# Projections beside the samples' cache pages: small factors, page weights and half of each page sum move from SBUF to PSUM, and the samples' softmax is reordered

## The chip, the cores and the metric

One core of a Trainium2 chip runs the whole program in one launch. The metric is device microseconds of that core, the median of several runs. Engines are called as in the profile: PE (TensorE), DVE (VectorE), ACT (ScalarE), POOL (GpSimd) and SP (SyncE, which issues most DMAs). Each engine takes its own instructions in the order written; engines wait for one another through semaphores.

## What is computed

The program is one step of a two-layer decoder for a prompt of 1024 tokens and for 8 samples of one token each. The change lies in the part between the two layers, where queries, keys, values and a gate are projected and where the samples attend to their cached pages. Cut to that part, the reference is:

```python
def shared_kv(x, kv_norm, kv_w, kv_fb, k_norm):
    u = rmsnorm(x, kv_norm) @ kv_w
    k = rmsnorm(u[..., :ATTN_DIM].reshape(b, t, N_HEADS, HEAD_DIM), k_norm)
    v = u[..., ATTN_DIM:2 * ATTN_DIM].reshape(b, t, N_HEADS, HEAD_DIM)
    logf = jax.nn.log_sigmoid((u[..., 2 * ATTN_DIM:] + kv_fb).astype(jnp.float32))
...
past_k = cache_k[page_table].reshape(bs, -1, N_HEADS, HEAD_DIM)   # 8 samples x 8 pages x 128 rows
past_v = cache_v[page_table].reshape(bs, -1, N_HEADS, HEAD_DIM)
...
def fox_mixer(x, k, v, cq, ck, q_pos, k_pos, norm_g, w_in, q_g, w_out):
    u = rmsnorm(x, norm_g) @ w_in
    q = rmsnorm(u[..., :ATTN_DIM].reshape(b, t, N_HEADS, HEAD_DIM), q_g)
    z = u[..., ATTN_DIM:]
    o = fox_attend(q, k, v, cq, ck, q_pos, k_pos).reshape(b, t, ATTN_DIM)   # softmax(q k / sqrt(d) + C[t] - C[s]) v
    return x + (o * jax.nn.silu(z)) @ w_out
```

There are 16 heads of 64 columns; a page holds 128 rows of 1024 columns of float32.

## The kernel before

The program has four stretches: the convolution layer (to about 467 us), the projections (467 to 973 us), the prompt's attention, and the output projection. The change touches the second.

**Eight steps of the projections.** `KINDS` names them: queries, keys, values and gate, each in two halves of 512 columns. Call them steps 0 to 7. Steps 0 to 5 run over eight tiles of 128 tokens; a tile is 24 matmuls of 512 columns into one PSUM bank (`pq`, L1105 to L1107). Its eight weight pieces (`wp`) are split into a high and a low part by ACT (L807) and DVE (L808) one step ahead, and the samples' own rows (`sample`, L883 and L884, 16 matmuls) come first in each step. Steps 6 and 7 (`gate`, L1053 to L1055) make the gate, four column blocks each.

**A tile's tail.** For queries and keys ACT copies the bank to `qn`, `head_rstd` makes eight factors per token (squares on ACT, L826; four small operations on DVE, L827, L830 to L832, with Ln and Exp on ACT between them), DVE multiplies the tile by them (L858), and three tiles later PE transposes the result (`ptq`, L872). For values ACT copies the bank to `vo`, and ACT (L848) and DVE (L849) split it into `vx`, which has two buffers and goes out by DMA.

**The samples' pages** run beside this. `keys` loads a page half (`kh`), multiplies it by the sample's query (L906; every fourth on DVE, the rest on POOL) and reduces it on DVE to logits in `lg` (L907). `softmax` turns the logits of four samples into weights, with small matmuls on PE between DVE's operations (`pm`, L984, L988, L998; `pd`, L1013). `values` loads both halves of a page (`vt`), multiplies them by the page's weights on DVE (L683) and adds them to `av` (L685; three quarters on POOL, a quarter on DVE); when a sample's eight pages are in, `fold` sums the rows by eight matmuls on PE (`pv`, L668). Samples 0 to 5 do this here, 6 and 7 in the output projection.

**The order.** `later_work` is a list of generators of which `pump2` takes APUMP[step] pieces (a page each) after each tile and ZPUMP after each block of the gate; `side` holds generators that advance by one piece at each `tick`. A scheduler then orders each engine's instructions by its own estimate of times. All eight PSUM banks of the stretch belong to one pool of eight (`psB1`).

Of the kernel before, what the change touches and what calls it, by code (L numbers as in the profile page):

```python
# [66 lines left out]
AP2 = 4  # L67
AP3 = 3
AP4 = 3
# [4 lines left out]
TLAG = 3  # L74
KHB = 6
# [24 lines left out]
ST = 2  # L100
# [34 lines left out]
def tile_step(ctx, tc, xt, st, stT, vecs, cwT, win, wout, wqkv, wf, wbo, hvec, qgf, ck, cv, cf, pt,  # L135
# [525 lines left out]
    def values(a, b, pool, kb, ab, bank):  # L661
        def fold(s_, av):
            while not bank:
                yield
            yield from [None] * FT
            pv = bank[0]("pv")
            for k in range(KT):
                PE.matmul(pv[:, k:k + 1], av[:, k * P:(k + 1) * P], ones[:, 0:1], start=True, stop=True)  # L668
            V.tensor_tensor(out=oT[:, :, s_], in0=pv[:, 0:KT], in1=oT[:, :, s_], op=ALU.add)
            folded.append(s_)  # L670

        for s_ in range(a, b):
            while s_ // 4 not in done or s_ - ab >= a and s_ - ab not in folded:
                yield
            av = pool.tile([P, D], F32, tag="av", name="av", bufs=ab)
            for g in range(NPG):
                i = s_ * NPG + g
                vt = [pool.tile([P, 512], F32, tag="kh", name="vt", bufs=kb) for _ in range(2)]
                fetch(i, *[(vt[x], cv, slice(x * 512, x * 512 + 512)) for x in range(2)])
                for x in range(2):  # L680
                    ax = av[:, x * 512:x * 512 + 512]
                    p0 = i * NH + x * 8
# [22 lines left out]
    with ExitStack() as pb:  # L705
# [6 lines left out]
        psB = pb.enter_context(tc.tile_pool(name="psB1", bufs=8, space=PSUM, reuse_waits="tile"))  # L712
# [21 lines left out]
        def gates():  # L734
            lfx = big("lfx")
            yield
            for o, n in CH:
# [7 lines left out]
                yield  # L745
            pl = bank("pl")
# [72 lines left out]
        def head_rstd(src, pn, nh, out):  # L819
            n = nh * HD  # L820
            sq = pX.tile([P, 512], F32, tag="hsq", name="hsq", bufs=2)
            v = sm.tile([P, 8], F32, tag="hv", name="hvv")
            y = sm.tile([P, 8], F32, tag="hv", name="hvy")
            a = sm.tile([P, 8], F32, tag="hv", name="hva")
            for h in range(nh):
                S.activation(out=sq[:pn, 0:HD], in_=src[:, h * HD:(h + 1) * HD], func=AF.Square, accum_out=v[:pn, h:h + 1])  # L826
            V.tensor_scalar(out=v[:pn, :nh], in0=v[:pn, :nh], scalar1=1.0 / HD, scalar2=EPS, op0=ALU.mult, op1=ALU.add)  # L827
            S.activation(out=y[:pn, :nh], in_=v[:pn, :nh], func=AF.Ln)
            S.activation(out=y[:pn, :nh], in_=y[:pn, :nh], func=AF.Exp, scale=-0.5)
            V.scalar_tensor_tensor(out=a[:pn, :nh], in0=y[:pn, :nh], scalar=-0.5, in1=y[:pn, :nh], op0=ALU.mult, op1=ALU.mult)  # L830
            V.tensor_tensor(out=a[:pn, :nh], in0=a[:pn, :nh], in1=v[:pn, :nh], op=ALU.mult)
            return V.scalar_tensor_tensor(out=out, in0=a[:pn, :nh], scalar=1.5, in1=y[:pn, :nh], op0=ALU.add, op1=ALU.mult)  # L832
# [3 lines left out]
        def token_tile(kind, half, t, ps):  # L836
            cs = slice(half * 512, (half + 1) * 512)
            if kind == 2:
                vo = wk.tile([P, 512], F32, tag="qn", name="vo", bufs=QNB)
                S.copy(out=vo, in_=ps)  # L840
                for x in range(2):

                    vx = pY.tile([P, 512], F32R, tag="tn", name="vx", bufs=TNB).rearrange("p (h a d) -> p h a d", h=4, a=2)
                    vi = heads(vo[:, x * 256:x * 256 + 256])
# [11 lines left out]
            r = sm.tile([P, 8], F32, tag="hr", name="hr")  # L856
# [22 lines left out]
        def sample(kind, half, ws):  # L879
# [9 lines left out]
            if kind < 2:  # L889
                r = sm.tile([P, 8], F32, tag="hr", name="hrs")  # L890
# [6 lines left out]
        def keys(half, a=0, b=NS):  # L897
            cs = slice(half * 512, (half + 1) * 512)
            for s_ in range(a, b):
                qb = pY.tile([P, 512], F32, tag="qb", name="qb", bufs=3)  # L900
                SY.dma_start(out=qb, in_=qs_scr[s_:s_ + 1, cs].broadcast_to([P, 512]))
                for g in range(NPG):
# [3 lines left out]
                    (V if g % 4 == 3 else G).tensor_tensor(out=kt, in0=kt, in1=qb, op=ALU.mult)  # L906
# [65 lines left out]

        def softmax(hf):
# [7 lines left out]
            yield from [None] * ST  # L981
# [4 lines left out]
            yield from [None] * ST  # L986
# [9 lines left out]
            yield from [None] * ST  # L996
# [14 lines left out]
            yield from [None] * ST  # L1011
# [22 lines left out]
        def new_row():  # L1034
            while not lns:
                yield
            ln = lns[0]
            nv = sample_rows(2)
            V.tensor_tensor(out=heads(nv), in0=heads(nv), in1=over_d(ln, NS, NH), op=ALU.mult)
            yield from [None] * NRT  # L1040
            pot = bank("pot")
            for k in range(KT):
                PE.transpose(pot[:, k * NS:(k + 1) * NS], nv[:, k * P:(k + 1) * P], ident[:NS, :NS])
# [25 lines left out]

        def started(hf):  # L1070

            while len(pieces_) < 4:
                yield
            side.append(softmax(hf))
# [5 lines left out]
        for n_, (kind, half) in enumerate(order):  # L1080
# [4 lines left out]
            if kind == 3:  # L1085
                if half:
                    pR.close()
                    load0()
                gate(half, ws)
                continue  # L1090
            sample(kind, half, ws)
            pieces_.append(n_)
            if n_ == 0:
                gate_work = gates()
                later_work.extend([page_gates(), keys(0)])
            if n_ == 1:
                later_work.extend([keys(1, 0, 4), started(0), keys(1, 4, NS), started(1), values(0, VB, pW, KHB, AVB, [bank])])
            if n_ == 2:
                side.append(page_bias())
            if n_ == 5:  # L1100
                side.append(new_row())
            for t in range(8):
                ps = bank("pq")
# [314 lines left out]
```

## Time and profile before

| | us |
|---|---|
| median of 3 runs | 1462.08 |
| runs | 1460.68, 1462.08, 1472.82 |
| the profiled execution | 1459.9 |
| its span, first to last instruction | 1458.2 |
| PE busy in it | 1292.8 (89%) |
| DVE, ACT, POOL busy | 1132.5 (78%), 734.1 (50%), 803.9 (55%) |

The span is what the trace shows; the execution's time is 1.7 us more, and the median of the runs is 2.2 us above this execution. Busy shares are means over stretches with different limits. PE's busy time includes time at a lowered clock, which the profile gives as a granted share of full speed.

### The profile page before, as it was taken

How to read it: one execution, taken by the hardware profiler on the slowest of the kernel's cores; microseconds unless marked ns; L12 is line 12 of the kernel's file. 1: busy time of each engine (PE TensorE's matmuls, PEld its weight loads, DVE VectorE, ACT ScalarE, POOL GpSimd, SP SyncE). 2: the span in 40 equal slices, each digit the busy share in tenths (PEclk: the TensorE clock that was granted, in tenths of full speed). 3: DMA queues.
4: the chain of work that ended last, by engine and by line, in shares of the span. 5: the costliest groups of instructions: out<-in, count | busy, mean ns of one | idle time of the engine just before them, and what ended most of it. 6: DMA issues, size and time to landing. Idle time of an engine off the chain costs nothing.

```text
span 1458.2 us, 21461 instructions
## 1 busy us (share of the span) xinstructions
PE 1292.8 (89%) x6543; PEld 1077.8 (74%) x6543; DVE 1132.5 (78%) x1844; ACT 734.1 (50%) x1922; POOL 803.9 (55%) x603
## 2 busy tenths in 40 slices
PE   5999999789999999998898899897988888887978
PEld 5999999777777777666776778786766666665766
DVE  6999999998735699989898999854656575667841
ACT  7676537646645666655642232135656565662100
POOL 4699987862210253456565565724545455567930
PEclk9999999999999999999998989997868798888979
DMA  5111001121334576878778888693444456423841
GB/s 206 56 59 59 30 29 34 30 75 41 130 125 145 158 225 203 229 250 272 231 251 273 277 272 268 211 241 91 111 96 101 92 133 133 101 48 118 286 139 37
DMA packets 155530, 213.95 MB, mean 147 GB/s; under 512 B 14057, under 2 KB 82281, under 8 KB 155399
## 3 DMA queue, kind: packets, MB, share of 16 engines
q1 hardware_dynamic: 137879, 202.09, 47.4%
q10 hardware_dynamic: 16896, 8.39, 2.0%
q0 software_dynamic: 640, 2.10, 0.5%
q8 instruction: 52, 0.85, 0.3%
q14 instruction: 63, 0.52, 0.1%
HBM read 165.22 MB, written 48.13 MB: 146 GB/s over the span
## 4 chain that ended last, share of the span: by engine, by line
PE 18%; DMA 10%; DVE 10%; issue 5%; SPq 4%; ACT 2%; POOL 1%; DVEq 0%; ACTq 0%; POOLq 0%
DMA k<-c_scr 4%; DVE vt L683 4%; DMA vt<-in_cv 3%; SPq L639 2%; PE st L1228 2%; PE st L1229 2%; PE ss L1166 2%; PE ss L1165 2%; DMA k<-kt_scr 2%; PE po L1208 1%; PE po L1209 1%; PE py L1312 1%; PE py L1314 1%; PE py L1313 1%; PE pz L1055 1%
## 5 line engine op out<-in xcount | busy, mean ns | idle before, releaser
L347 POOL TENSOR_TENSOR cvt<-cvt 128x512 f32<-128x512 f32 (+4 forms) x179 | 243.7, 1394 | 38.4 <-ACT cvt L343 35.5
L906 POOL TENSOR_TENSOR kh<-kh,qb 128x512 f32<-128x512 f32 x96 | 139.8, 1472 | 135.6 <-DMA kh<-in_ck 85.4
L352 DVE SCALAR_TENSOR_TENSOR acc<-u,cw,acc 128x512 f32<-128x512 f32 (+4 forms) x285 | 196.0, 742 | 0.1
L198 POOL TENSOR_SCALAR ph<-pt 128x896 fp32r<-128x896 f32 (+1 forms) x96 | 87.6, 921 | 175.9 <-ACT pt L1238 172.3
L1169 DVE TENSOR_REDUCE nm<-ss 128x1 f32<-128x768 f32 (+7 forms) x128 | 93.6, 751 | 110.4 <-PE ss L1168 97.5
L685 POOL TENSOR_TENSOR av<-av,vt 128x512 f32<-128x512 f32 x80 | 134.2, 1698 | 69.8 <-DVE vt L683 53.0
L1105 PE MATMUL pq<-wp,acth 128*128 128x512 f32 x384 | 160.1, 417 | 0.0
L1107 PE MATMUL pq<-wp,actl 128*128 128x512 f32 x384 | 156.4, 407 | 0.0
L1106 PE MATMUL pq<-wp,acth 128*128 128x512 f32 x384 | 156.2, 407 | 0.0
L683 DVE TENSOR_TENSOR vt<-vt,lg 128x512 f32<-128x512 f32 x112 | 133.8, 1228 | 7.8 <-DMA vt<-in_cv 7.6
L343 ACT ACTIVATE cvt<-u,cw 128x512 f32<-128x512 f32 (+4 forms) x195 | 126.1, 719 | 17.9 <-POOL cvt L347 9.4
L1171 ACT ACTIVATE ss<-ss,nm 128x768 f32<-128x768 f32 (+7 forms) x128 | 91.2, 713 | 44.5 <-DVE nm L1169 43.4
L1238 ACT ACTIVATE pt<-st 128x896 f32<-128x896 f32 (+1 forms) x96 | 75.4, 809 | 71.7 <-PE st L1229 46.6
L1242 POOL TENSOR_TENSOR pl<-pt,ph 128x384 fp32r<-128x384 f32 (+2 forms) x56 | 105.7, 1894 | 2.7
L1165 PE MATMUL ss<-k,q 128*128 128x512 f32 (+2 forms) x192 | 80.2, 425 | 23.7 <-DMA k<-kt_scr 14.6
L1166 PE MATMUL ss<-k,q 68*128 68x512 f32 (+2 forms) x192 | 74.3, 400 | 20.4 <-DMA k<-c_scr 17.7
L1107 PEld LDWEIGHTS pq<-wp,actl 128*128 128x128 f32 x384 | 75.2, 196 | 19.2 <-issue 0.8
L1105 PEld LDWEIGHTS pq<-wp,acth 128*128 128x128 f32 x384 | 75.8, 197 | 18.0 <-ACT hsq L826 0.8
L1106 PEld LDWEIGHTS pq<-wp,acth 128*128 128x128 f32 x384 | 75.7, 197 | 16.9 <-issue 0.2
L907 DVE TENSOR_REDUCE lg<-kh 128x8 f32<-128x512 f32 x128 | 82.7, 673 | 5.0 <-POOL kh L906 5.0
L1208 PE MATMUL po<-ph,vh 128*128 128x512 f32 x192 | 78.3, 411 | 5.8 <-DVE og L1213 4.0
L1228 PE MATMUL st<-q,k 128*128 128x512 f32 (+1 forms) x192 | 79.5, 422 | 3.0 <-ACT ss L1171 2.9
(337 smaller groups left out, 3788.7 us busy)
## 6 DMA issues: line engine op xcount, KB each, us to landing
kh<-in_ck SPq DMA_DIRECT2D x128, 256.0 KB
vt<-in_cv SPq DMA_DIRECT2D x128, 256.0 KB
wraw<-in_wqkv SPq DMA_DIRECT2D x56, 256.0 KB
wr<-in_win SPq DMA_DIRECT2D x24, 512.0 KB
q<-qt_scr SPq DMA_DIRECT2D x48, 256.0 KB
k<-kt_scr SPq DMA_DIRECT2D x48, 256.0 KB
vt_scr<-vx SPq DMA_DIRECT2D x32, 256.0 KB
vh<-vt_scr SPq DMA_DIRECT2D x16, 512.0 KB
```

Source lines behind the costliest of these rows:

```text
L343: S.activation(out=t[:, :m], in_=u[:, lo + j:hi + j], func=AF.Copy, scale=cw[:, c, j:j + 1])
L347: G.tensor_tensor(out=pacc[:, :m], in0=pacc[:, :m], in1=t[:, :m], op=ALU.add)
L352: V.scalar_tensor_tensor(out=acc, in0=u[:, lo + jd:hi + jd], scalar=cw[:, c, jd:jd + 1], in1=acc, op0=ALU.mult, op1=ALU.add)
L683: V.tensor_tensor(out=heads(vt[x] if g else ax), in0=heads(vt[x]), in1=over_d(lg[:, p0:p0 + 8], P, 8), op=ALU.mult)
L685: (V if g % VDVE == 3 else G).tensor_tensor(out=ax, in0=ax, in1=vt[x], op=ALU.add)
L906: (V if g % 4 == 3 else G).tensor_tensor(out=kt, in0=kt, in1=qb, op=ALU.mult)
L1105: PE.matmul(ps, na.hi(k, t * P, P), ws[k][:, 0:512], start=(k == 0), stop=False)
L1106: PE.matmul(ps, na.hi(k, t * P, P), ws[k][:, 512:1024], start=False, stop=False)
L1107: PE.matmul(ps, na.lo(k, t * P, P), ws[k][:, 0:512], start=False, stop=(k == KT - 1))
L1165: PE.matmul(ss[:, b0:b0 + w], q1[:, qsl], k1[:, b0:b0 + w], start=True, stop=False)
L1228: PE.matmul(st[:, o:o + w], k1[:, js], q1[:, qs], start=(o % 512 == 0), stop=False)
L1242: (G if plo else V).tensor_tensor(out=pl[:, :off], in0=pt_[:, :off], in1=f32(ph[:, :off]), op=ALU.subtract)
```

## The change

It does the following. One PSUM bank (`smb`) takes the small tiles of `head_rstd` and a copy of a sample's page weights; another (`a2`) takes the second half of a sample's page sum, whose additions all go to DVE, those of the first half all to POOL, and ACT copies `a2` back to `av` at the end. The pool for projection banks shrinks from eight to six. In `head_rstd` one of DVE's four small operations becomes a Square on ACT, and what remains reads at most one SBUF tile. The value tile's split reads the projection's bank instead of `vo`. For keys DVE multiplies every eighth page instead of every fourth. The samples' own rows of steps 1 to 5 come after the second tile instead of ahead of the first. The logits of samples 0 to 3 are finished in both halves first, the softmax of them starts when they are in, its pieces stand three ticks apart instead of two (fewer in the gate), and the page counts per tile are 3, 3, 3, 4, 4, 3 instead of 3, 3, 4, 3, 3, 3. The samples' new value row is loaded in two halves of another pool.

```diff
-AP2 = 4
-AP3 = 3
-AP4 = 3
+AP2 = 3
+AP3 = 4
+AP4 = 4
...
+SPOS = 2
...
-ST = 2
+ST = 3
...
-    def values(a, b, pool, kb, ab, bank):
+    def values(a, b, pool, kb, ab, bank, small=None, psA=None):
...
+            wt, w0 = lg, s_ * NPG * NH
+            if small is not None:
+                wt, w0 = small(NPG * NH), 0
+                V.tensor_copy(out=wt, in_=lg[:, s_ * NPG * NH:(s_ + 1) * NPG * NH])
+            a2 = av[:, 512:1024] if psA is None else psA.tile([P, 512], F32, tag="a2", name="a2")
...
-                    V.tensor_tensor(out=heads(vt[x] if g else ax), in0=heads(vt[x]), in1=over_d(lg[:, p0:p0 + 8], P, 8), op=ALU.mult)
+                    ax = a2 if x else av[:, 0:512]
+                    p0 = w0 + g * NH + x * 8
+                    V.tensor_tensor(out=heads(vt[x] if g else ax), in0=heads(vt[x]), in1=over_d(wt[:, p0:p0 + 8], P, 8), op=ALU.mult)
                     if g:
-                        (V if g % VDVE == 3 else G).tensor_tensor(out=ax, in0=ax, in1=vt[x], op=ALU.add)
+                        (V if (g % VDVE == 3 if psA is None else x) else G).tensor_tensor(out=ax, in0=ax, in1=vt[x], op=ALU.add)
                 yield
+            if psA is not None:
+                S.copy(out=av[:, 512:1024], in_=a2)
...
-        psB = pb.enter_context(tc.tile_pool(name="psB1", bufs=8, space=PSUM, reuse_waits="tile"))
+        psB = pb.enter_context(tc.tile_pool(name="psB1", bufs=6, space=PSUM, reuse_waits="tile"))
+
+        psm = pb.enter_context(tc.tile_pool(name="psM", bufs=1, space=PSUM, reuse_waits="tile"))
+        smb = psm.tile([P, 512], F32, name="smb")
...
+            yield
             pl = bank("pl")
...
-            v = sm.tile([P, 8], F32, tag="hv", name="hvv")
-            y = sm.tile([P, 8], F32, tag="hv", name="hvy")
-            a = sm.tile([P, 8], F32, tag="hv", name="hva")
+            v, y2, a = [small(8)[:pn, :nh] for c in "vya"]
+            w, y = [sm.tile([P, 8], F32, tag="hw", name="hw" + c)[:pn, :nh] for c in "vy"]
...
+            V.tensor_scalar(out=w, in0=v, scalar1=1.0 / HD, scalar2=EPS, op0=ALU.mult, op1=ALU.add)
+            S.activation(out=y, in_=w, func=AF.Ln)
+            S.activation(out=y, in_=y, func=AF.Exp, scale=-0.5)
+            S.activation(out=y2, in_=y, func=AF.Square)
+            V.scalar_tensor_tensor(out=a, in0=y2, scalar=-0.5, in1=w, op0=ALU.mult, op1=ALU.mult)
+            return V.scalar_tensor_tensor(out=out, in0=a, scalar=1.5, in1=y, op0=ALU.add, op1=ALU.mult)
...
-                    vi = heads(vo[:, x * 256:x * 256 + 256])
+                    vi = heads(ps[:, x * 256:x * 256 + 256])
...
-            r = sm.tile([P, 8], F32, tag="hr", name="hr")
+            r = small(8)
...
-                    (V if g % 4 == 3 else G).tensor_tensor(out=kt, in0=kt, in1=qb, op=ALU.mult)
+                    (V if g % NPG == 7 else G).tensor_tensor(out=kt, in0=kt, in1=qb, op=ALU.mult)
...
+        def hop(n):
+
+            while n > 0:
+                yield
+                n -= 1 + gating[0]
...
-            yield from [None] * ST
+            yield from hop(ST)
...
-            while len(pieces_) < 4:
+            while len(pieces_) < 4 or hf not in counts or hf and 0 not in done:
                 yield
-            side.append(softmax(hf))
+            yield from softmax(hf)
...
-            if n_ == 1:
-                later_work.extend([keys(1, 0, 4), started(0), keys(1, 4, NS), started(1), values(0, VB, pW, KHB, AVB, [bank])])
...
             for t in range(8):
+                if t == SPOS and n_:
+                    sample(kind, half, ws)
+                    pieces_.append(n_)
+                if t == SPOS and n_ == 1:
+                    later_work.extend([keys(1, 0, 4), counted(0), keys(0, 4, NS), keys(1, 4, NS), counted(1), values(0, VB, pW, KHB, AVB, [bank], small, psA)])
```

Three places show what this does to the engines' order. On DVE, in the tail of a key tile (`hvv`, `hvy`, `hva`, `hr` are the small factors, `smb` the new bank, `hwv` and `hwy` two that stay in SBUF), before:

```order
L827 TENSOR_SCALAR hvv<-hvv 128x8
L830 SCALAR_TENSOR_TENSOR hva<-hvy 128x8
L831 TENSOR_TENSOR hva<-hva,hvv 128x8
L832 SCALAR_TENSOR_TENSOR hr<-hva,hvy 128x8
L858 TENSOR_TENSOR qn<-qn,hr 128x512
L907 TENSOR_REDUCE lg<-kh 128x8 x3
```

and now:

```order
L848 TENSOR_SCALAR hwv<-smb 128x8
L852 SCALAR_TENSOR_TENSOR smb<-smb,hwv 128x8
L853 SCALAR_TENSOR_TENSOR smb<-smb,hwy 128x8
L879 TENSOR_TENSOR qn<-qn,smb 128x512
L928 TENSOR_REDUCE lg<-kh 128x8 x3
```

The row with two SBUF factors into a third (L831) is gone, and each of the others reads one operand from PSUM. On DVE, among the page weights' products of step 5, before:

```order
L849 TENSOR_TENSOR vx<-vo,vx 128x4x64
L683 TENSOR_TENSOR vt<-vt,lg 128x512 x5
L685 TENSOR_TENSOR av<-av,vt 128x512
L849 TENSOR_TENSOR vx<-vo,vx 128x4x64
L683 TENSOR_TENSOR vt<-vt,lg 128x512
L985 TENSOR_REDUCE m_5007<-pm 128x4
```

and now, where a new sample begins:

```order
L691 TENSOR_TENSOR a_9477<-a_9477,vt 128x512
L680 COPY smb<-lg 128x128
L689 TENSOR_TENSOR av<-vt,smb 128x512
L689 TENSOR_TENSOR a_9727<-vt,smb 128x512
L689 TENSOR_TENSOR vt<-vt,smb 128x512
L870 TENSOR_TENSOR vx<-pq,vx 128x4x64
L689 TENSOR_TENSOR vt<-vt,smb 128x512
L691 TENSOR_TENSOR a_9727<-a_9727,vt 128x512
```

The products read the weights from the bank, the sum of the second half (`a_9477`, `a_9727`) stands in PSUM, and one of DVE's additions comes with each page. On PE, at the seam from step 5 to the gate, before:

```order
L1107 MATMUL pq<-wp,actl 128x512
L998 MATMUL pm_10270<-dmm,ones 128x64
L668 MATMUL pv<-ones,av 128x1 x8
L1053 MATMUL pz<-acth,wp 128x512
L1054 MATMUL pz<-actl,wp 128x512
```

and now:

```order
L1148 MATMUL pq<-wp,actl 128x512
L1027 MATMUL pm_10344<-dmm,ones 128x64
L669 MATMUL pv<-ones,av 128x1 x4
L1084 MATMUL pz<-acth,wp 128x512
L1085 MATMUL pz<-actl,wp 128x512
```

The page sum at this seam was the second sample's, and it is the third's now (in two groups of four matmuls, of which the first stands here); the first sample's has moved from after the fifth tile of step 5 to after the third.

## Rows read from the trace of the kernel before

**Rows 1.** Windows: steps 0 to 2, steps 3 to 5, gate. Width, busy us by engine, PEclk, DMA share, GB/s.

```profile
467.00:670.00 203.00, 188.71 (x882) 142.10 (x880) 173.87 (x327) 129.54 (x552) 92.80 (x68) 0.96 0.73 216
670.00:857.00 187.00, 163.45 (x691) 129.02 (x691) 169.55 (x255) 76.65 (x282) 107.86 (x71) 0.91 0.85 265
857.00:973.00 116.00, 107.28 (x679) 96.60 (x680) 95.59 (x110) 23.55 (x54) 64.61 (x39) 0.93 0.82 243
```

**Rows 2.** What PE waited for, 467 to 973 us: total us, times, longest.

```profile
PE pm L998 <- ACT le L994: 7.4, 1, 7.4
PE pz L1055 <- DVE wp L808: 6.9, 1, 6.9
PE ptq L872 <- DVE qn L858: 6.4, 5, 2.9
PE pss L884 <- DVE wp L808: 6.4, 2, 4.0
PE pm L988 <- DVE m L985: 5.8, 2, 4.4
...
PE pl L749 <- DVE lfx L744: 3.5, 1, 3.5
```

**Rows 3.** Groups of instructions, 467 to 973 us: busy us, mean ns, idle before.

```profile
L906 POOL TENSOR_TENSOR kh<-kh,qb 128x512 f32<-128x512 f32 x96 | 139.8, 1472 | 135.6 <-DMA kh<-in_ck 85.4 <-DMA qb<-qs_scr 23.4 <-DVE lgw L765 8.1
L685 POOL TENSOR_TENSOR av<-av,vt 128x512 f32<-128x512 f32 x60 | 101.0, 1704 | 66.7 <-DVE vt L683 49.9 <-PE pz L1055 10.0 <-DVE av L685 2.5
L683 DVE TENSOR_TENSOR vt<-vt,lg 128x512 f32<-128x512 f32 x84 | 93.2, 1135 | 7.1 <-DMA vt<-in_cv 6.8
...
L858 DVE TENSOR_TENSOR qn<-qn,hr 128x512 f32<-128x512 f32 x32 | 28.4, 888 | 0.7
L906 DVE TENSOR_TENSOR kh<-kh,qb 128x512 f32<-128x512 f32 x32 | 28.3, 885 | 1.6 <-DMA qb<-qs_scr 1.6
...
L849 DVE TENSOR_TENSOR vx<-vo,vx 128x256 fp32r<-128x256 f32 x32 | 22.0, 693 | 1.8 <-ACT vx L848 1.8
...
L685 DVE TENSOR_TENSOR av<-av,vt 128x512 f32<-128x512 f32 x24 | 20.0, 844 | 1.4 <-POOL av L685 1.2
...
L827 DVE TENSOR_SCALAR hvv<-hvv 128x8 f32<-128x8 f32 x32 | 14.9, 466 | 1.9 <-ACT hsq L826 1.7
...
L831 DVE TENSOR_TENSOR hva<-hva,hvv 128x8 f32<-128x8 f32 x32 | 13.1, 411 | 0.7
...
L830 DVE SCALAR_TENSOR_TENSOR hva<-hvy 128x8 f32<-128x8 f32 x32 | 11.3, 353 | 7.0 <-ACT hvy L829 7.0
L832 DVE SCALAR_TENSOR_TENSOR hr<-hva,hvy 128x8 f32<-128x8 f32 x32 | 10.1, 314 | 0.8
...
L828 ACT ACTIVATE hvy<-hvv 128x8 f32<-128x8 f32 x32 | 6.7, 208 | 62.0 <-DVE hvv L827 58.5 <-DVE hva L831 3.5
```

**Rows 4.** DVE in order of time, 843 to 846 us: start, us.

```profile
843.27 1.78 DVE L683 TENSOR_TENSOR vt<-vt,lg 128x512 f32<-128x512 f32 x1
...
845.05 0.68 DVE L683 TENSOR_TENSOR vt<-vt,lg 128x512 f32<-128x512 f32 x1
```

**Rows 5.** DVE by tile and line: ns min/median/max, first and last start.

```profile
L888 DVE TENSOR_TENSOR sr<-pss,st x6: 671/672/679, 486.2 to 822.5; 8x512 f32<-8x512 f32 x6
...
L669 DVE TENSOR_TENSOR oT<-pv,oT x6: 157/160/173, 845.0 to 962.2; 128x8 f32<-128x8 f32 x6
...
L875 DVE SCALAR_TENSOR_TENSOR tnl<-ptq,qg,tnh x32: 729/739/752, 513.2 to 919.6; 128x512 fp32r<-128x512 f32 x32
...
L849 DVE TENSOR_TENSOR vx<-vo,vx x32: 401/414/1516, 753.8 to 894.7; 128x256 fp32r<-128x256 f32 x32
```

**Rows 6.** Three windows of 15 us, columns as in rows 1.

```profile
485.00:500.00 15.00, 15.00 (x99) 12.66 (x100) 7.81 (x18) 13.81 (x56) 0.00 (x0) 1.00 0.43 128
800.00:815.00 15.00, 15.00 (x67) 12.16 (x66) 15.00 (x19) 5.50 (x9) 8.12 (x5) 1.00 0.96 304
920.00:935.00 15.00, 8.09 (x51) 7.56 (x50) 12.24 (x16) 0.98 (x2) 11.43 (x6) 0.77 0.60 175
```

More of the change, by code (lines that the diff above doesn't have):

```diff
@@ L889, in sample @@
             if kind < 2:
-                r = sm.tile([P, 8], F32, tag="hr", name="hrs")
+                r = small(8)
                 head_rstd(src, NS, 8, r[:NS])
@@ L971, in tile_step @@
         done = []
+        def hop(n):
+            while n > 0:
+                yield
+                n -= 1 + gating[0]
+        gating = [0]
         def softmax(hf):
@@ L985, in softmax @@
             V.tensor_reduce(out=m1[:, ss], in_=pm.rearrange("p (s t) -> p s t", s=4), axis=AX.X, op=ALU.max)
-            yield from [None] * ST
+            yield from hop(ST)
             pm = bank("pm2")
@@ L995, in softmax @@
             mm = spread(mx, "m")
-            yield from [None] * ST
+            yield from hop(ST)
             pm = bank("pm3")
@@ L1010, in softmax @@
             ld_ = spread(le, "d")
-            yield from [None] * ST
+            yield from hop(ST)
             pd = bank("pd")
@@ L1034, in new_row @@
         def new_row():
-            while not lns:
+            while not lns or len(pieces_) < 6:
                 yield
             ln = lns[0]
-            nv = sample_rows(2)
-            V.tensor_tensor(out=heads(nv), in0=heads(nv), in1=over_d(ln, NS, NH), op=ALU.mult)
-            yield from [None] * NRT
+            nv = [wk.tile([NS, 512], F32, tag="qn", name="nv", bufs=QNB) for _ in range(2)]
+            for x in range(2):
+                SY.dma_start(out=nv[x], in_=rows_s[2][:, x * 512:x * 512 + 512])
+                V.tensor_tensor(out=heads(nv[x]), in0=heads(nv[x]), in1=over_d(ln[:, x * 8:x * 8 + 8], NS, 8), op=ALU.mult)
+            yield from hop(NRT)
             pot = bank("pot")
             for k in range(KT):
-                PE.transpose(pot[:, k * NS:(k + 1) * NS], nv[:, k * P:(k + 1) * P], ident[:NS, :NS])
+                PE.transpose(pot[:, k * NS:(k + 1) * NS], nv[k // 4][:, k % 4 * P:k % 4 * P + P], ident[:NS, :NS])
             V.tensor_tensor(out=oT, in0=oT, in1=pot[:, 0:KT * NS].rearrange("p (k s) -> p k s", k=KT), op=ALU.add)
@@ L1068, in gate, with counted @@
                 tick()
+        counts = []
+        def counted(hf):
+            counts.append(hf)
+            yield from ()
         def started(hf):
-            while len(pieces_) < 4:
+            while len(pieces_) < 4 or hf not in counts or hf and 0 not in done:
                 yield
-            side.append(softmax(hf))
+            yield from softmax(hf)
         pieces_ = []
```

26 lines of the change are left out of this document (13 added, 13 removed).

## The prediction

> **What bounds the kernel now.** I read the page's slices first: the change touches only the stretch from 467 to 973 us, and PE is busy nearly throughout it. So the next view is the busy time by window [rows 1]. Its first two columns after the bounds are the width and PE's busy time; their difference is PE's idle time: 203 - 188.7 = 14.3 us in steps 0 to 2, 187 - 163.5 = 23.6 us in steps 3 to 5, 116 - 107.3 = 8.7 us in the gate, 46.6 us together. The clock column adds a second loss, hidden in the busy time: 0.96, 0.91 and 0.93 of full speed cost 4%, 9% and 7% of the widths, 8, 17 and 8 us. The two go together. In a window in which PE had no gap the clock was 1.00; in one with 6.9 us of gaps it was 0.77 [rows 6], which of the two levels, 2.4 and 1.2 GHz, means nearly half the window at the lower. So the most that the stretch could give back is 46.6 + 33 = some 80 us.
>
> Then, who causes the gaps: in the list of PE's waits nearly all releasers are DVE, or ACT behind DVE: softmax steps (7.4 and 5.8), weight pieces not yet split (6.9 and 6.4), tiles not yet normalised (6.4), the forget gates' rows (3.5) [rows 2]. DVE is busy 173.9 of 203 and 169.6 of 187 us [rows 1]: an engine with a queue, in which what PE needs stands behind page work.
>
> Why DVE is so full is in the groups [rows 3]. The same product of a page with its weights takes 0.68 us at 845.05 and 1.78 us at 843.27 [rows 4], 1.135 on the mean, and operations on eight columns take 0.31 to 0.47 [rows 3]. All read two SBUF tiles (or are a tensor_scalar), and POOL works in these stretches. Operations of the same sizes with one operand in PSUM never show it: 671 to 679 ns for 512 columns, 729 to 752 over 32 instructions, 157 to 173 for eight [rows 5].
>
> **The change, part by part.** First DVE's load. Products: 96 for samples 0 to 5, of which the 84 into `vt` fall from 1.135 to 0.68, saving 38 us. Factors: four groups of 32, 14.9 + 13.1 + 11.3 + 10.1 = 49.4 us, become three of 0.16, 15.4 us, saving 34. The multiplication by them, 28.4 us, becomes 32 x 0.69 = 22, saving 6. The value split, 22.0 us, becomes 32 x 0.414 = 13, saving 9. Keys: 16 of 32 products at 0.885 go to POOL, saving 14. Added: 42 sums at 0.68 for 24 at 0.844, +8.6, and six copies of weights, about 0.2 each, +1 [rows 3, 5]. Net: some 90 us less of 439. POOL gets 112 products of keys for 96 and 42 sums for 60: at the present means of 1.472 and 1.704 us that is 236 us for 241 [rows 3], and less as far as DVE no longer holds it up. ACT gets 36 Squares at 0.208, 7.5 us [rows 3], and six copies of 512 columns, at most 0.7 each by DVE's price for that size. Both lie in ACT's free half (230 of 506 us busy [rows 1]), and ACT now spends 62 us waiting for DVE ahead of the Ln [rows 3]. If that cover were gone they would cost their 12 us.
>
> The rule against this: the Trainium skill, Perfetto Trace Analysis, section Optimizing Scalar/DVE Operations, gives DVE an overhead of about 60 ns on SBUF and 125 ns on PSUM. By it the roughly 320 operations that get a PSUM operand would pay 21 us, DVE would win 70 and not 90, and the first term below would be 12 and not 15. The 671 ns with a PSUM operand [rows 5] beside 0.68 us without one [rows 4] speak against it, so I leave it out of the sum.
>
> *Steps 0 to 2* (queries and half the keys). Of 14.3 us of gaps the 3.5 of the forget gates get one more tile of slack from the added yield, and about 6 of late tiles and weights shrink with DVE's queue; the rest, with the first weights of the stretch, stays. I take 10 of 14.3 and 5 of the 8 us of clock: 15. The samples' rows after the second tile are the same 16 matmuls in another place. They no longer need the last weight piece within 3.6 us of a step's start (16 matmuls at 15/67 = 0.224 us [rows 6]) but tile 0 needs it within 5.4. Bounds: 5 (a weight piece is still late in each step) and 22 (all of it).
>
> *Steps 3 to 5* (the other keys, the values). Here DMA is the second limit. It moves 265 GB/s at a share of 0.85 now [rows 1], 304 at 0.96 in the best window shown [rows 6]. The counts per tile give these steps 88 pieces instead of 72: of the 131 pieces of keys and logits 59 remain for them (51 before), and 29 pieces of values (21 before). Eight more key pages of 262 KB and eight more value pages of 524 KB are 6.3 MB on top of 265 x 187 = 49.6 MB. Not all must be in: the third page sum stands on PE at the end of step 5 and needs 24 value pages, 2.6 MB less. 53.3 MB take 201 us at 265 GB/s and 175 at 304. PE's own floor is 187 - 23.6 - 17 = 146. I take 300 GB/s, near the best window, since buffers come free sooner when DVE and POOL are not in each other's way: 178 us, 9 less than now. So the softmax waits of 7.4 and 5.8 us go [rows 2], with DVE's queue and the third tick of slack, and what is late next is the page sums: PE's order has the second three tiles (16 us) after the first, and the third two tiles (11 us) after that, while eight value pages alone, 4.2 MB, take 14 us of all DMA engines at 300 GB/s, and a tile's own 0.8 MB of values comes on top. Bounds: -14 (201) and +41 (146).
>
> *Gate.* Values need 19 more pieces there instead of 27. The 6.9 us wait for one weight piece behind page products should go, and the half of a clock stretch behind it; the other 1.8 us may stay. I take 11 of 17, bounds 0 and 17. The attention's first 16 loads move ahead of the last pages on SP's queue; the page loads behind them come later by their issue, but only the last page sums wait for those, and PE has gate blocks of 12 us between them. Cost nothing, or up to 8 us if the sums are then last.
>
> *Elsewhere* the order of instructions does not change.
>
> Sum: 15 + 9 + 11 = 35 us. The profiled execution took 1459.9, so it would take 1425; the median of the runs is 2.2 us above it, so 1427.
>
> **The rivals.** *Pages bind* (22%): DMA stays at 265 GB/s, steps 3 to 5 last 195 to 201 us with gaps in front of the page sums, and only steps 0 to 2 and the gate gain: 15 + 11 - 11 = 15, 1447. For it: DMA's share is 0.85 there already, and POOL waited 85 us for key pages [rows 3]. Against it: the best window had 304 GB/s with DVE 15.0 of 15 us busy [rows 6].
>
> *PE alone binds* (15%): the page sums come in time because the first samples' values start in step 4 and are buffered; then all but 12 of the 80 us come back, 1394. For it: the clock is 1.00 wherever PE has no gap [rows 6]. Against it: 53 MB in 150 us would be 355 GB/s, above any window.
>
> *Six banks* (8%), slower than before: a value tile now keeps its bank until DVE has made both halves of `vx`, and there are six. A tile takes PE 24 x 0.224 = 5.4 us. The last split of `vx` is at 894.7 [rows 5], 38 us after PE left step 5 at 857, seven tiles behind; six banks allow some 30. Unchanged, that costs 8 us; with the page stream 14 us later in the same DVE queue, 22 us, and with gaps at every tile the clock of steps 4 and 5 (some 100 us) falls to 0.77, 14 more. 36 - 15 - 11 = 10: 1472, up to 1485 if the first term goes too. It decides from the point at which the split lags PE by more than 30 us. Against it: the split's median is 0.41 us where its mean is 0.69 [rows 3, 5], and DVE's queue shortens. The Trainium skill (Perfetto Trace Analysis, Matmul Optimizations) asks for all eight banks to be in use; by it this rival would be the forecast, and no row here shows PE waiting for a bank.
>
> **How the numbers follow.** My forecast, 1412 to 1441 around 1427, has 55%. The range must reach into "pages bind" and some of the way to "PE alone binds": 1398 to 1456 leaves out most of the slow rival, a part of the pages rival and the best half of the PE rival, 2 in 10. One per cent, which is what a measurement of this kernel tells from no change, is 14.6 us: faster than 1447.5 are the forecast, the PE rival and a good third of the pages rival, 79%; slower than 1476.7 is half of the slow rival, 4%; the rest, 17%, lies between.
>
> **What would show it.** Right: products of pages at 0.68 us throughout, DVE some 90 us less busy in the stretch, POOL's sums nearer to 1.47 than to 1.70; in the list of PE's waits the softmax lines and the weight piece in the gate gone or under 2 us, and a wait for page sums in step 5 in their place; DMA near 300 GB/s in steps 3 to 5; attention beginning about 35 us earlier and as long as before. Wrong: PE's first matmul of a value tile waiting for ACT or DVE (the banks), products still at 1.1 us (PSUM operands do contend), or attention longer by what the projections saved.

## The result, and the profile after

The changed kernel takes 1474.8 us (median of 20 runs, 1461.8 to 1482.4) against 1464.3 us for the kernel before on the same chips. The ratio is 1.007, 95% interval 1.0048 to 1.0093: it is slower, and the prediction of 1427 us is missed on the wrong side. The profiled execution of the changed kernel spans 1460.1 us, against 1458.2 us for the one of before. It is the fastest of the changed kernel's 20 runs, 13 us below their median, so the rows below show the mechanisms and understate what the change costs in a run of median length.

First the windows of the changed kernel over the same three stretches, which answer to [rows 1] (width, busy us of PE, PEld, DVE, ACT and POOL, PEclk, DMA share, GB/s):

```profile
467.00:670.00 203.00, 185.87 (x876) 142.43 (x877) 138.99 (x288) 132.19 (x576) 89.76 (x72) 0.96 0.74 212
670.00:857.00 187.00, 156.20 (x683) 121.59 (x682) 141.27 (x259) 77.19 (x299) 101.53 (x78) 0.92 0.87 275
857.00:973.00 116.00, 104.39 (x652) 93.08 (x651) 69.78 (x118) 23.62 (x51) 33.50 (x26) 0.93 0.78 233
```

DVE fell from 173.9, 169.6 and 95.6 us to 139.0, 141.3 and 69.8, and PE gained nothing by it. Its idle time is the width less the busy time: 17.1 us in steps 0 to 2 (14.3 before), 30.8 in steps 3 to 5 (23.6), 11.6 in the third window (8.7). Who causes it is in the waits of PE from 467 to 973 us, which answer to [rows 2]:

```profile
PE ptq L893 <- DVE qn L879: 27.8, 7, 12.6
PE pv L669 <- POOL av L691: 23.7, 3, 11.9
PE pn L567 <- ACT xn L564: 3.3, 1, 3.3
PE pss L904 <- ACT wp L829: 2.8, 1, 2.8
PE pq L1147 <- DVE wp L830: 2.5, 1, 2.5
...
PE pl L771 <- DVE lfx L765: 0.7, 1, 0.7
```

The softmax lines and the gate's weight piece are gone and the forget gates' rows are at 0.7 us, as forecast. In their place stand two lines, 51.5 us together: PE waits for a normalised tile (`ptq`, 6.4 us before) and for page sums (`pv`, not in the list before). All of the first lies ahead of 738 us, where step 4 begins, and all of the second behind it.

How long the stretch lasts is in the starts of PE's matmuls (count, ns min/median/max, first and last start), the first of step 0 and the first and last of the gate, before:

```profile
L1105 PE MATMUL pq<-wp,acth x384: 388/395/795, 470.5 to 849.8; 128*128 128x512 f32 x192
L1053 PE MATMUL pz<-acth,wp x192: 277/284/774, 857.3 to 973.1; 128*128 128x512 f32 x64, 128*128 128x256 f32 x64, 128*128 128x264 f32 x64
L1055 PE MATMUL pz<-acth,wp x192: 277/283/796, 858.3 to 973.3; 128*128 128x512 f32 x64, 128*128 128x256 f32 x64, 128*128 128x264 f32 x64
```

and now:

```profile
L1146 PE MATMUL pq<-wp,acth x384: 388/395/776, 471.7 to 860.2; 128*128 128x512 f32 x192
L1084 PE MATMUL pz<-acth,wp x192: 278/284/774, 873.4 to 978.5; 128*128 128x512 f32 x64, 128*128 128x256 f32 x64, 128*128 128x264 f32 x64
L1086 PE MATMUL pz<-acth,wp x192: 274/283/628, 874.4 to 978.8; 128*128 128x512 f32 x64, 128*128 128x256 f32 x64, 128*128 128x264 f32 x64
```

From the first of these starts to the last, the stretch took 502.8 us before and takes 507.1 now.

The groups of instructions from 467 to 973 us, which answer to [rows 3], show that each operation did become as cheap as the prediction says:

```profile
L927 POOL TENSOR_TENSOR kh<-kh,qb 128x512 f32<-128x512 f32 x112 | 147.2, 1335 | 139.6 <-DMA kh<-in_ck 61.9 <-DMA qb<-qs_scr 42.4 <-DVE hwv L848 10.6
...
L847 ACT ACTIVATE hsq<-qn 128x64 f32<-128x64 f32 x256 | 65.6, 256 | 43.8 <-DVE qn L879 29.2 <-DVE sr L913 4.6 <-ACT hsq L847 4.5
L689 DVE TENSOR_TENSOR vt<-vt,smb 128x512 f32<-128x512 f32 x84 | 56.1, 680 | 20.1 <-DMA vt<-in_cv 19.4 <-POOL av L691 0.3
L691 POOL TENSOR_TENSOR av<-av,vt 128x512 f32<-128x512 f32 x42 | 54.4, 1295 | 94.5 <-DVE vt L689 85.0 <-DVE mb L1029 2.9 <-issue 1.9
...
L691 DVE TENSOR_TENSOR a<-a,vt 128x512 f32<-128x512 f32 x42 | 29.1, 692 | 0.4
L879 DVE TENSOR_TENSOR qn<-qn,smb 128x512 f32<-128x512 f32 x32 | 21.9, 684 | 0.9
...
L870 DVE TENSOR_TENSOR vx<-pq,vx 128x256 fp32r<-128x256 f32 x32 | 13.2, 414 | 5.9 <-ACT vx L869 5.9
...
L849 ACT ACTIVATE hwy<-hwv 128x8 f32<-128x8 f32 x32 | 6.7, 208 | 14.6 <-DVE hwv L848 14.6
...
L852 DVE SCALAR_TENSOR_TENSOR smb<-smb,hwv 128x8 f32<-128x8 f32 x32 | 5.3, 167 | 11.2 <-ACT smb L851 10.9
L848 DVE TENSOR_SCALAR hwv<-smb 128x8 f32<-128x8 f32 x32 | 5.1, 160 | 16.9 <-ACT hsq L847 16.6
```

Page products are at 680 ns (1135), factors at 160 to 170 (314 to 466), the multiplication at 684 (888). The row to stop at is the second: ahead of its squares ACT is idle 29.2 us behind `DVE qn L879`, a wait that is 0.3 us in the kernel before. ACT's list of waits for the whole stretch, the samples' squares included, has it with its count:

```profile
ACT hsq L847 <- DVE qn L879: 33.4, 17, 7.7
```

The timeline shows one of these 17 (start, us, and the wait in brackets), rows of DVE, ACT and PE:

```profile
613.35 0.15 DVE L853 SCALAR_TENSOR_TENSOR smb<-smb,hwy 128x8 f32<-128x8 f32 x1
...
613.66 0.68 DVE L879 TENSOR_TENSOR qn<-qn,smb 128x512 f32<-128x512 f32 x1
...
614.38 0.26 ACT L847 ACTIVATE hsq<-qn 128x64 f32<-128x64 f32 x1 [3.63 <-DVE qn L879]
...
614.49 0.45 PE L893 MATMUL ptq<-ident,qn 128*128 128x128 f32 x1 [5.31 <-DVE qn L879]
```

DVE finishes one tile's multiplication at 614.34. At that moment two engines start at once: PE its transposes of that tile, and ACT the first square of the *next* tile, which reads nothing of it. What ties the two tiles together is `smb`: the squares add into it, the multiplication reads it, and its slots are 32 sets of eight columns, so that no tile uses a slot of the tile before. The program orders the two engines' uses of this bank as a whole, not by columns: in the trace 36 of the 288 squares carry a wait for DVE, as many as there are tiles (32) and groups of samples (4). In the kernel before 4 do.

### The profile page after: what moved, and what is told of

Read it like the earlier page. It is cut to its first block, busy times and chain, and to the rows that moved or that the text cites. A ratio compares the mean times of both kernels' runs of the same rounds, so it can differ in the third digit from the quotient of the medians.

```text
span 1460.1 us, 21524 instructions
## 1 busy us (share of the span) xinstructions
PE 1278.0 (88%) x6543; PEld 1066.3 (73%) x6543; DVE 1046.3 (72%) x1817; ACT 737.6 (51%) x1964; POOL 761.9 (52%) x601
## 5 line engine op out<-in xcount | busy, mean ns | idle before, releaser
L927 POOL TENSOR_TENSOR kh<-kh,qb 128x512 f32<-128x512 f32 x112 | 147.2, 1335 | 139.6 <-DMA kh<-in_ck 61.9
L1146 PE MATMUL pq<-wp,acth 128*128 128x512 f32 x384 | 157.4, 410 | 0.0
L1147 PE MATMUL pq<-wp,acth 128*128 128x512 f32 x384 | 154.3, 402 | 2.5 <-DVE wp L830 2.5
L691 POOL TENSOR_TENSOR av<-av,vt 128x512 f32<-128x512 f32 x62 | 87.1, 1414 | 97.6 <-DVE vt L689 88.1
L344 ACT ACTIVATE cvt<-u,cw 128x512 f32<-128x512 f32 (+4 forms) x195 | 126.0, 718 | 17.6 <-POOL cvt L348 9.3
L1207 PE MATMUL ss<-k,q 68*128 68x512 f32 (+2 forms) x192 | 73.0, 394 | 23.7 <-DMA k<-c_scr 18.3
L1147 PEld LDWEIGHTS pq<-wp,acth 128*128 128x128 f32 x384 | 74.3, 193 | 19.0 <-DVE wp L830 3.0
L847 ACT ACTIVATE hsq<-qn 128x64 f32<-128x64 f32 x256 | 65.6, 256 | 43.8 <-DVE qn L879 29.2
```

What stands on the lines that cost most here:

```text
L344: S.activation(out=t[:, :m], in_=u[:, lo + j:hi + j], func=AF.Copy, scale=cw[:, c, j:j + 1])
L927: (V if g % NPG == 7 else G).tensor_tensor(out=kt, in0=kt, in1=qb, op=ALU.mult)
L1146: PE.matmul(ps, na.hi(k, t * P, P), ws[k][:, 0:512], start=(k == 0), stop=False)
L1147: PE.matmul(ps, na.hi(k, t * P, P), ws[k][:, 512:1024], start=False, stop=False)
L1207: PE.matmul(ss[:, b0:b0 + w], q2[0:HD + 4, qsl], k2[0:HD + 4, b0:b0 + w], start=False, stop=not lastb)
```

## The experiments

Three theories, by the letters of the expectations. **Theory A:** the one small bank ties ACT's squares to DVE's multiplication, so the tiles' tails run one after the other and PE's transposes come late. **Theory B:** page sums stand on PE before their pieces are there. **Theory D:** the new order fills DVE's queue, and that alone delays the tails. Ratios are to the kernel before, with 95% intervals.

Beside each ratio stands the *length* of the stretch in the profiled execution, from the first matmul of step 0 to the last of the gate as above (502.8 us before, 507.1 now). It is needed because an edit in the stretch can also move what lies outside of it. Behind the gate PE, DVE and ACT take their instructions in the same order in the kernel before and in the changed kernel, and from the gate's last matmul to the first of the output projection pass 360.7 and 360.1 us; in e1 the scheduler placed some of those instructions in another order, and it is 350.5. Over the experiments it lies between 346 and 363 us, apart from e8. The ratio includes that, the length doesn't.

### e1: the factors of the two engines apart

```diff
-            v, y2, a = [small(8)[:pn, :nh] for c in "vya"]
-            w, y = [sm.tile([P, 8], F32, tag="hw", name="hw" + c)[:pn, :nh] for c in "vy"]
+            w, a = [small(8)[:pn, :nh] for c in "wa"]
+            v, y, y2 = [sm.tile([P, 8], F32, tag="hw", name="hw" + c, bufs=8)[:pn, :nh] for c in "vyz"]
```

> The changed kernel, but what ScalarE writes of the small factors (the sums of the squares and the square of the root) lies in SBUF; only what VectorE alone writes (w, a, r) stays in the small PSUM bank, so a tile's first square no longer has to wait for the multiplication of the tile before it. Theory A (each tile's tail is serialised by the one bank, and PE's transposes come late): the 33.4 us in which ScalarE's squares wait for VectorE's product fall under 8, PE's waits at ptq fall from 27.8 us to under 10, and the time is 0.990 to 0.998 of the kernel before (the changed kernel stands at 1.007). Theory B (the page sums stand too early in PE's order): the waits at ptq may go, but pv keeps its 24 us or grows, and the time stays at 1.002 to 1.008. Theory D (the new order fills VectorE's queue and that alone delays the tails): the squares' waits go, ptq keeps 20 us or more, 1.005 to 1.009.

Measured: 0.988 (0.9832 to 0.9928), 1442.9 us, further than theory A asked. PE's waits of e1 over 467 to 973 us:

```profile
PE pv L669 <- POOL av L691: 18.5, 3, 10.1
PE ptq L893 <- DVE qn L879: 5.7, 2, 3.5
PE ptq L893 <- ACT hsq L847: 5.7, 2, 5.4
```

ACT's wait for the multiplication, 33.4 us, is not in its list at all any more (2 of the 288 squares carry a wait for DVE), and the waits at `ptq` fell from 27.8 to 11.4 us, against under 10 expected. ACT is idle ahead of the Ln instead, 41.4 us for 16.2, behind DVE's first operation on the same tile. DVE's operations kept their prices (684 ns for the multiplication). The length fell from 507.1 to 493.3 us. So the tie is shown, and these 13.8 us are its price in the stretch. The step in the ratio, from 1.007 to 0.988, is some 28 us, and the rest of it is not shown to be the tie's: in the two profiled executions 9.6 us lie in the attention with its other order. Theory D, by which `ptq` would stay, falls for this kernel. Of the wait at `pv` 18.5 of 23.7 us stay, as B said, though the time is not the one that B gave.

### e2: all tile factors in SBUF

`head_rstd` and `r` as in the kernel before, the rest as changed.

> The changed kernel with all small factors of the tiles back in SBUF as in the kernel before (page weights and half of each page sum stay in PSUM). Theory A: the squares' waits for VectorE vanish as in e1, ptq waits under 12 us, but 32 products of qn take up to 1.78 us again where GpSimd works beside them, at most 35 us of VectorE's time, which has slack: 0.993 to 1.002 of before, a little behind e1. Theory B: pv waits of 20 us or more stay, 1.002 to 1.008. Theory D: ptq waits of 20 us or more stay, 1.005 to 1.010.

Measured: 1.0054 (1.0023 to 1.0084), outside what I gave for A. It lies where B and D put it, but the waits of 20 us or more that each of them asked for are 15.7 us at `pv` and 15.4 at `ptq`. The wait for the multiplication is gone, but DVE is busy 405 us from 467 to 973 us instead of 350, and the length is 507.6 us, no shorter than the changed kernel's. I had counted on DVE's slack to take the dearer operations (982 ns for the multiplication); it does not. That this is so because they stand in the tiles' tails is likely, and no run tests it. So the factors in PSUM have their worth, once the two engines' are apart: e1 is 1.7% ahead, 14.3 us in length.

### e3: pages in SBUF, factors as changed

`values(...)` called without `small` and `psA`, seven banks for PE.

> The changed kernel with the page weights and the page sums in SBUF as in the kernel before and the freed bank given back to PE (7 instead of 6); the tiles' small factors stay in PSUM. Theory A: the tails stay serialised (squares wait 30 us or more), ptq waits of 20 us or more in steps 1 to 3 stay, and VectorE has some 45 us more of products from step 4 on: 1.005 to 1.015 of before. Theory B: the pieces come by DMA as late as they did, pv waits of 15 to 30 us stay: 1.004 to 1.012. If the half sum on ScalarE and VectorE in PSUM is what makes pv late, pv waits fall under 10 us and the time falls to 0.996 to 1.002.

Measured: 1.0022 (0.9987 to 1.0056). The squares still wait 33.2 us for the multiplication, `ptq` 25.6 us in two lines, `pv` 29.6. The time came out below both ranges; its interval overlaps that of the changed kernel, so it does not tell them apart. The lengths do: 520.9 us against 507.1. The pages' part in PSUM is worth 13.8 us in the stretch, against one bank more for PE, and the time hides it, since in e3 the attention, in another order of instructions, is just as much shorter (346.3 against 360.1 us).

### e4: the new order alone

Nothing in PSUM but eight banks for PE; factors, values and the shares of keys as before; the order as changed.

> Nothing in PSUM but PE's banks (8), the values' copies and the share of the key products as in the kernel before; of the change only the new order is left (samples two tiles later, softmax from step 3 on, counts 3,3,3,4,4,3, new rows later). Theory A: squares don't wait for VectorE, ptq waits under 10 us, the softmax waits stay gone: 0.995 to 1.001 of before. Theory B: pv waits of 20 us or more as in the changed kernel, 1.000 to 1.008. Theory D: the losses are all here, ptq waits of 20 us or more, 1.005 to 1.012.

Measured: 1.019 (1.0152 to 1.0228), slower than any theory said; length 534.4 us. PE's waits of e4 over 467 to 973 us:

```profile
PE pv L669 <- DVE av L691: 33.0, 3, 15.1
PE ptq L881 <- DVE qn L867: 22.1, 6, 6.7
PE pot L1062 <- DVE nv L1058: 8.7, 1, 8.7
```

The squares wait for no multiplication here, so the 22.1 us at `ptq` come with the order as well, on a DVE that is as full as before (435 us busy, 439 before, with 6.4 us at `ptq` [rows 2]): theory D holds where nothing is in PSUM. The 33.0 us at `pv` come with the order, and not with PSUM.

### e5 and e6: the old order

e5 is the kernel before with `head_rstd`, `values`, the two PSUM pools, the value split and the key shares of the change. e6 is e5 with e1's two lines.

> The kernel before, in its old order (counts, samples, softmax, new rows), with all that the change keeps in PSUM and the keys' products shared as in the change. Together with e4 (the order alone, 1.019 of before) and the changed kernel (both, 1.007) this is the fourth corner. Theory A (one bank serialises the tails): the squares wait 25 us or more for VectorE, and PE waits 15 us or more at ptq; if the parts in PSUM are worth the same in either order, 0.985 to 0.995 of before, since 1.007 over 1.019 is 0.988. If the order alone was the loss and the bank costs nothing, 0.975 to 0.985. If the order pays only with the parts in PSUM, 1.000 to 1.015.

> As e5, with the small factors parted as in e1: ScalarE's in SBUF, VectorE's in the small bank. Theory A: the squares' waits for VectorE vanish here too, and e6 over e5 is 0.975 to 0.990, as e1 over the changed kernel was (0.988 over 1.007, 0.981). If the new order is a loss as in e4, e6 comes out ahead of e1: 0.970 to 0.984 of before. If the new order is worth what it saves at the softmax once VectorE has room, e6 is behind e1: 0.990 to 1.000.

Measured: e5 0.9897 (0.9843 to 0.995), e6 0.9804 (0.9754 to 0.9854). In e5 the squares wait 33.1 us in 23 cases and PE 31.1 us at `ptq`; in e6 the first is gone and the second is 12.5. `pv` is at 2.5 us in e5 and not in e6's list. e6 over e5 is 0.991, just outside the 0.975 to 0.990 that theory A gave. All six corners, as ratios to before and as lengths in us:

| order | nothing in PSUM | as changed | e1's factors apart |
|---|---|---|---|
| old | 1; 502.8 | 0.9897; 492.2 (e5) | 0.9804; 478.1 (e6) |
| new | 1.019; 534.4 (e4) | 1.007; 507.1 | 0.988; 493.3 (e1) |

Read along the rows, the parts in PSUM are worth 1.0 and 1.2% (10.6 and 27.3 us in length), and parting the factors 0.9 and 1.9% more. By the lengths the parting is worth the same in both orders, 14.1 and 13.8 us. Read down the columns, the new order costs 1.9, 1.7 and 0.8%, in length 31.6, 14.9 and 15.2 us. The measured change is a gain and a larger loss.

### e7 and e11: page sums later on PE

```diff
-FT = 1
+FT = 2
```

That is e7; e11 has 3.

> e1 with each sample's page sum put one more tile later in PE's order (FT 2 instead of 1). Theory B (page sums stand too early in PE's order and DMA brings the pieces late): PE's waits at pv fall from 18.5 us to under 6 us, VectorE's wait for pv goes too, and the time is 0.978 to 0.985 of before. Rival: each tile later only moves the piece that PE waits for, since the next sample's pieces may not start before the sum two samples back is done; then pv keeps 12 us or more, or the last samples' sums run on behind the gate, and the time is 0.986 to 0.995.

> e1 with the page sums two tiles later (FT 3), counts as in the change. Theory B in its form of a place on PE's queue: pv waits 18.5 us (FT 1), 8.5 us (FT 2), under 3 us here; 0.976 to 0.983 of before. Rival (the pieces of the sample after next may not start before the sum is done, since there are two sum buffers): pv waits go, but the last samples' pieces start later and fall into the gate, whose end moves back by 5 us or more against e7 (960 us): 0.984 to 0.992.

Measured: e7 0.9827 (0.9781 to 0.9873), e11 0.9791 (0.9749 to 0.9833). The waits at `pv` of e7, and then of e11:

```profile
PE pv L669 <- POOL av L691: 8.5, 3, 3.8
```

```profile
PE pv L669 <- POOL av L691: 1.1, 1, 1.1
```

18.5, 8.5 and 1.1 us with each tile later. e7's 8.5 is over the 6 that I gave, since the pieces are more than one tile late. The length is 493.3 us in e1, 481.3 in e7 and 469.1 in e11, and the last gate matmuls start at 969.4, 960.0 and 940.8 us: the rival, by which held-back pieces would push the gate's end out, fell. The edit is one number. The scheduler then moved some of DVE's and ACT's instructions too, but the wait shrinks with each tile and the length with it, so B is shown: the sums stood too early. It is what the new order cost once the factors were apart: e11's time is level with that of e6 (0.979 and 0.980), which has the old order and no wait at `pv`, and its length is 9.0 us less.

### e8, e9 and e10: when the pieces are issued

The counts of pieces per tile in e1: 3,3,4,3,3,3 as before in e8, 3,3,4,4,3,3 in e9, and e9 with FT 2 in e10.

> e1 with the counts of page pieces per tile of the kernel before (3,3,4,3,3,3 instead of 3,3,3,4,4,3): one piece more in each tile of step 2, one less in those of steps 3 and 4. Theory B: the pieces ask less of DMA in steps 3 and 4 and the page sums stand later, so pv waits fall from 18.5 to under 10 us; 0.980 to 0.987 of before. Rival (the pieces of step 2 are what VectorE has no room for): ptq waits in steps 2 and 3 grow from 11 to over 18 us, and the time is 0.988 to 1.000.

> e1 with as many page pieces in all, but the steps of four are steps 2 and 3 instead of 3 and 4 (3,3,4,4,3,3). Theory B as the runs so far leave it (PE waits at pv because four pieces a tile in step 4, with the samples' tail behind them, ask for more than DMA brings, and the page sums follow in PE's row): with three pieces a tile from step 4 on the row of pieces catches up before the first page sum, pv waits fall from 18.5 us to under 8 us, the projections end some 8 to 12 us sooner than in e1 (969 us), and the time is 0.976 to 0.984 of before. Rival (the sum's place in PE's order alone decides, one tile behind its last piece): pv keeps 12 us or more, 0.985 to 0.992. Second rival (VectorE has no room for a fourth piece in step 2): ptq waits in step 2 grow by over 8 us, 0.986 to 0.996.

> e9 with the page sums one tile later as well (FT 2), so both remedies for pv. Theory B: pv waits under 3 us, 0.972 to 0.982 of before, at or below e9 and e7 (0.983). Rival: one remedy does all that there is to do, and this is level with the better of e7 and e9, within 0.003.

Measured: e8 1.0026 (0.9989 to 1.0064), e9 0.9819 (0.9781 to 0.9858), e10 0.9794 (0.9749 to 0.9839). In e8 `pv` fell to 0.8 us and the length to 478.3 us, 15 us less than in e1, yet the run was longer: e8 lost it in the attention (389.0 us against 350.5), to something that neither theory had. ACT's groups from 960 us on:

```profile
L1222 ACT ACT_TABLE_LOAD x32 | 41.1, 1283 | 0.6
L1212 ACT ACT_TABLE_LOAD x22 | 28.2, 1283 | 2.3 <-issue 1.9
...
L1279 ACT ACT_TABLE_LOAD x11 | 14.1, 1283 | 9.5 <-PE st L1270 9.3
```

In this order a Silu of the gate landed behind the load of the attention's table (949.2 us, the Silu's own load follows at 950.5), and ACT then changed tables 65 times, 83 us. No other kernel here does, so e8's time says nothing of the counts. e9 answers the question without that: `pv` is at 5.5 us, the length is 482.6 us, and the time is in B's range. e10 has under 3 us at `pv`, a length of 476.1 us, and is level with e11, so after either remedy the other adds nothing that these intervals show. From 670 to 857 us DMA moves 282 GB/s in e1, 287 in e9, 290 in e10 and 295 in e11: the stream of pages is faster where PE waits less.

### e12: the pages' part in PSUM, with tails clean

e1 with e3's edit.

> e1 with the page weights and page sums in SBUF as in the kernel before, and one more bank for PE (7): the small factors' share of the gain by itself, in the new order. If the pages' part in PSUM is worth its 45 us of VectorE time: VectorE's busy time in the gate's window (857 to 973 us) rises by 25 us or more, pv waits grow over 22 us, and the time is 0.993 to 1.003 of before, 7 us or more behind e1. If it is worth nothing, since the pieces come by DMA no faster (e3 against the changed kernel said so, 1.002 to 1.007): level with e1, 0.985 to 0.991.

Measured: 1.0016 (0.9985 to 1.0047), 1.4% behind e1; length 513.7 us, 20.4 more than e1's. DVE in the third window has 88.3 us instead of 63.9, a rise of 24.4 where 25 were expected, and PE waits 30.8 us at `pv` and 14.4 at `ptq`. So the pages' part is worth its place in PSUM with clean tails too, and by the lengths more than with tied ones (20.4 us against 13.8 in e3).

## Why the prediction was wrong

**Right.** DVE's load: 90 us less forecast, 439.0 to 350.1 measured, part by part (the products fell 37 us, 38 forecast; factors are 15.8 us, 15.4 forecast). POOL's sums are cheaper, as forecast, at 1295 ns. Softmax and weight piece are gone from PE's waits, the forget gates are at 0.7 us. The gate by itself: 116.1 us became 105.4, 10.7 less where the term said 11. The order elsewhere did not change: from the gate's last matmul to the first of the output projection it is 360.7 us before and 360.1 after.

The three terms beside what the traces show, by the first matmul of each step (us saved against the kernel before; 3.6 us of the first row belong to the second, by the prediction's 0.224 us a matmul, since step 3's 16 matmuls for the samples have moved from ahead of the step into it):

| | forecast | changed kernel | e1 (no tie) | e11 (no tie, sums later) |
|---|---|---|---|---|
| steps 0 to 2 | 15 | 7.5 | 18.5 | 17.6 |
| steps 3 to 5 | 9 | -22.5 | -17.6 | 1.4 |
| gate | 11 | 10.7 | 8.6 | 14.7 |
| sum | 35 | -4.3 | 9.5 | 33.7 |

**The step that failed first: "Both lie in ACT's free half".** I weighed the new Squares by ACT's busy time, and took the 62 us that ACT waited for DVE as cover. That wait did shrink, from 62.0 to 14.6 us ahead of the Ln, but the change put a new one ahead of the first square of each tile (33.4 us). I had shown where the factors go and priced each, and had not asked which engine writes into the bank after which has read it. The Trainium skill, PSUM — Partial Sum Buffer, section PSUM bank collisions raise a hardware error, says that two engines' accesses are to be guarded by the bank (and its quarter of the partitions) and not by the address. The 33.4 us of squares that wait for another tile's columns agree, and the kernel without them (e1) gives their price. So "*Steps 0 to 2*: 15" and a part of "*Steps 3 to 5*" rested on tails that get faster, while their tie took back 13.8 us of length, 10.9 of them in steps 0 to 2: that term gave 7.5 us, and 18.5 without the tie. The prediction's own figure for lost cover, 12 us, is near the 13.8 by chance: it was the price of the added ACT instructions, not of a wait.

**The step that failed second, and cost more: the term of 9 for steps 3 to 5.** Its reasoning was right: "what is late next is the page sums", and the lower bound was -14. Its value was taken from 300 GB/s, "since buffers come free sooner", with no term for PE standing at a sum. The stretch ran at 275 in the changed kernel, and at 295 where nothing else was in the way (e11). Of 9 us forecast the traces show 22.5 lost, and 17.6 still without the tie; with the sums two tiles later it is 1.4 gained. With the tie's share the start of the gate, forecast 24 us sooner, came 16.1 us later. With both faults mended (e11) it is at 839.4, 17.9 us sooner.

**The rivals.** *Pages bind* had the second mechanism's sign, gaps in front of the page sums; its 1447 us lacked the tie, and e1, without it, took 1443. But DMA did not stay at 265 GB/s, and e11 shows that the sums' place on PE, not DMA alone, made the gaps. *Six banks* was on the right side for the wrong reason. All eight banks are in use in the changed kernel too, six of them by PE's pool, and PE's longest wait inside a value tile's row is the 2.5 us at `pq L1147`, for a weight piece. *PE alone binds* is shown wrong by `pv`.

With e1's two lines and FT 3 the same change gives 0.979 (0.9749 to 0.9833), 1434.1 us, the best of these kernels with e10 (0.979) and e6 (0.980). My 1427 is 0.975 of 1464.3: the sum of 35 us is nearly what e11's stretch gives, 33.7, though by luck in part, since the terms differ. What it left out is what the change did to itself.

**Left open:** why the scheduler's other order makes the attention of e1, e3 and e12 10 to 14 us shorter than the changed kernel's; and which of the new order's parts besides the sums costs or pays, since e11 and e6, level in time, were not mixed. That the changed kernel's median stands 13 us over its own profiled execution is no riddle of this kernel: its 20 runs spread over 20 us, and e5's and e11's profiled executions are 13 and 11 us below their medians.

## What to carry to other kernels

Before small tiles of several engines go into one PSUM tile, list for each write which engine last read that tile: here two lines that gave each engine's results their own place took some 14 us off the stretch in either order. An engine's idle time is no cover until it is known what its next instruction waits for. A result that another engine consumes in order should be placed in that engine's row by when its inputs land under full load, and a remedy is to be judged by the stretch that it changes and not by the whole time alone: the pages' part was worth 20.4 us of length in e12's pair and 13.8 in e3's, where the time showed nothing, because a scheduler also moved the instructions behind.

## What the runs showed of the hardware

A gap on PE can cost again after it has ended. Two windows of 15 us of the changed kernel, with columns as in [rows 1]:

```profile
600.00:615.00 15.00, 8.20 (x31) 6.60 (x32) 12.79 (x24) 6.58 (x28) 2.51 (x2) 0.77 0.83 227
...
724.00:739.00 15.00, 15.00 (x66) 12.22 (x65) 12.83 (x25) 9.79 (x45) 9.06 (x8) 0.88 0.83 261
```

The second has no gap at all and a mean granted clock of 0.88, so that a quarter of it passed at the lower of the two levels, 1.2 and not 2.4 GHz; the gap of 12.6 us at `ptq` had ended at 723.6 us. [Rows 6] showed the loss only in a window that itself had gaps, and the prediction's "the clock is 1.00 wherever PE has no gap" does not hold here.

A table load on ACT took 1283 ns, and the order of one Silu against it decided whether the attention's table came once or ACT changed tables 65 times (e8).

An operand in PSUM made none of these DVE operations dearer: 680 ns for 512 columns, 414 for 256, 160 to 170 for eight, where the medians with two SBUF operands before were 692 (the multiplication), 414 and 166 to 168. What went away is the slow instances. The changed kernel holds both kinds, since samples 6 and 7 still read their page weights from `lg` in SBUF (ns min/median/max, first and last start):

```profile
L689 DVE TENSOR_TENSOR vt<-vt,smb x84: 616/679/690, 801.4 to 944.7; 128x512 f32<-128x512 f32 x84
...
L689 DVE TENSOR_TENSOR vt<-vt,lg x28: 676/1752/1787, 1341.2 to 1400.4; 128x512 f32<-128x512 f32 x28
```

The Trainium skill, Perfetto Trace Analysis, section Optimizing Scalar/DVE Operations, gives DVE about twice the overhead on PSUM that it gives on SBUF; the rows of this kernel do not show that, and the 350.1 us of DVE are what came of leaving it out.
